# A decoder step on one core: row sums applied by a job of their own, decode attention's values in one burst of matmuls, and matmuls of that stretch tied to places in TensorE's order

## The chip, the cores and the metric

The kernel runs on one core of a Trainium2 chip. The metric is the time of one execution on the device, in microseconds (us). In the profile PE is TensorE, PEld its weight loads, DVE is VectorE, ACT is ScalarE, POOL is GpSimd, SP is SyncE, which here only issues DMAs; a name with a q (SPq) is the queue of that engine, where it waits before it issues. Every engine works through its own instructions in order, and a program that runs at build time decides that order.

## The reference, cut to what matters

One step of a one-layer decoder: 1024 prompt rows and 8 decode rows of width 2048 go through one input projection, sparse attention, an mLSTM and an output projection, all in fp32.

```python
(aq, ak, av, iq, ik, iw, az, mq, mk, mv, mi, mf, mo, mz) = jnp.split(h @ w_in, split_points, axis=-1)

def sparse_attend(q, kg, vg, valid):              # kg, vg: the rows that the index chose
    logits = jnp.einsum('bqhgd,bqjhd->bqhgj', qg, kg) * ATT_SCALE      # 8 heads, 2 kv heads, 128 wide
    p = jax.nn.softmax(jnp.where(valid, logits, -jnp.inf), axis=-1)
    return jnp.einsum('bqhgj,bqjhd->bqhgd', p, vg).reshape(B, Q, ATT_WIDTH)

def dsa_sample(...):                              # 8 decode rows, each chooses 256 of 4097 positions
    _, idx = lax.top_k(scores, topk)
    kg = jnp.where(in_past, cache_k[phys, off], new key)               # paged cache
    vg = jnp.where(in_past, cache_v[phys, off], new value)
    return sparse_attend(q, kg, vg, valid)
# attention's output * silu(az), beside the mLSTM's * silu(mz), goes through w_out; then x + that, RMSNorm
```

## The kernel before, in words

Each fp32 operand is split into a high and a low part, and a product of tiles is three matmuls: high by high, high by low, low by high. The splits of a weight tile (`wraw`, 128x512) are one cast on ACT (L222, tile `wH`) and one subtraction on DVE (L223, tile `wL`), into rings of three buffers each.

**The projection.** The input projection has 61 tiles of 128 columns. Tiles up to 36 are made one after the other by `mm` (L1376, the matmul is L1385) in four quarters of 36 matmuls each; the last two, 35 and 36, run their quarters in the order 2, 3, 0, 1. The activations that these matmuls read are the tiles `xP` (256 columns) and `xQ` and `xR` (388 columns). Tiles 37 to 60 are 12 pairs, made in two phases: 24 steps, numbered 0 to 23, by a product with seven multiplications instead of eight (L1620). Its weights are loaded on the SP queue (L1592, L1595, L1598) into fixed slots and a ring, some are added by a DMA on the POOL queue (L1604), and DVE and ACT split them (L1609, L1610). Steps 0 to 11 store partial sums, and steps 12 to 23 load them back (`pfetch`, L1638, tile `xR` or `ev`) and finish the tiles. Steps 20 to 23 finish the eight tiles of attention's gate az.

**The jobs.** Beside the projection two lanes of jobs are stepped once per quarter. Each job has a first and a last tile and a weight, and a lane runs each job so that its yields come at an even pace between these tiles. On lane 0 the index job chooses positions, the job `att` is the prompt's attention, and `ml` the mLSTM; on lane 1 stand the decode rows' parts. A list scheduler at build time then puts all instructions in order, engine by engine; instructions that are given to `pin` keep the order in which the program issues them.

**Decode attention** (`job_datt`, L1214) runs late in the tiles before 37, after the index job. Sixteen times DVE multiplies a gathered tile of keys `kv` by the query and reduces it (L1264, L1268) into a column group of `lT`. PE then transposes `lT` (L1276), softmax runs on DVE and ACT, PE transposes P (L1296), and 32 matmuls of 4 columns (L1309; an fp32 matmul leaves two records, so the trace has 64) apply the gathered values. The gathers are indirect DMAs on POOL (L1236) into a ring of six buffers. `att` starts when it is done: L577 transposes its values, L614 and L615 are its first softmax.

**Row sums.** `att` writes its output to `attS` in device memory undivided, and the reciprocals of its row sums to `rcS`. They are applied in steps 20 to 23: for each output piece `out` loads them, broadcast over partitions, into a buffer `rb` of the five-buffer ring `ev` (L1665, 24 loads on SP); `use` multiplies the projection's result by them (L1740), takes tanh on ACT (L1744), combines on DVE (L1745) and stores the gate to `gateS` on the POOL queue (L1746), from the same ring. At the end `mixload` reads attention and gate for the output projection (L1352, L1356).

Of the kernel before, what the change touches and what calls it, by code (L numbers as in the profile page):

```python
# [8 lines left out]
F32 = mybir.dt.float32  # L9
# [4 lines left out]
OP = mybir.AluOpType  # L14
# [4 lines left out]
S = 1024  # L19
NB = 8  # L20
# [127 lines left out]
def body(tc, A, stop=None):  # L148
# [1068 lines left out]
    def job_datt():  # L1217
        with tc.tile_pool(name="da", bufs=1, side="right") as pd:
# [37 lines left out]
            for b in range(NB):  # L1256
# [43 lines left out]
            yield 4000  # L1300
            po = bank()
            for b in range(NB):
                if b + 2 < NB:
                    vgs.append(gather("cv", b + 2))
                vg = vgs.pop(0)
                for v in range(2):
                    o = b * 8 + v * 4
                    for u in range(2):
# [3 lines left out]
            ot = pd.tile([128, 8, NB], F32, name="ot")  # L1312
# [4 lines left out]
            V.tensor_tensor(ot, po[:, :64].rearrange("p (b h) -> p h b", b=NB), kn.rearrange("p b h -> p h b"), OP.add)  # L1317
            for x in range(2):
                SY.dma_start(attS[x][:, S:R].rearrange("(a p) b -> p a b", p=128), ot[:, x * 4:x * 4 + 4])
            yield 3000  # L1320

    def att_free():
# [5 lines left out]
    def ix_weight(blocks):  # L1328
# [10 lines left out]
                   Job("dsel", T_AK, 30.0, 2000 + 31 * 1700 + 10000 + 16 * 2800 + 2000, job_dsel),  # L1339
                   Job("datt", T_MQ, 35.5, 7500 + 8 * 5000 + 4000 + 8 * 2500 + 3000, job_datt, ix_free),  # L1340
                   Job("dml", T_G + 0.25, T_G + 10, 20000 + 16 * 2500 + 5000, job_dml)])]
    gateV = gateS.rearrange("(k p) r -> k p r", p=128)
# [280 lines left out]
    keep = {}  # L1623
    parts, free = {}, []
    ahead = [(v, x, c) for v, (_, n) in enumerate(seq) if any(m == n for _, m in seq[:v])
# [14 lines left out]

    def pump(v):
        while free and ahead and ahead[0][0] <= v:
            pfetch()

    def out(v, x, c, ps, sv=None, eng=SC):
# [4 lines left out]
        if not second(v):  # L1650
# [9 lines left out]
            return  # L1660
        rb = None
        if t >= T_AZ:
            cp = min(cn, S - c0)
            rb = evp.tile([128, CN], F32, name="ev")
            SY.dma_start(rb[:, :cp], rcS[(t - T_AZ) // 4][(t - T_AZ) % 4, c0:c0 + cp].partition_broadcast(128))  # L1665
        if (x, c) == (0, 1):
            if t < T_G:
                e = evp.tile([128, CN], F32, name="ev")
                SC.activation(e[:, :cn], ps[:, :cn], AF.Copy, scale=mk)
            else:  # L1670
                e = ps
            use(n, x, c, e, rb)
            return
# [28 lines left out]

    def use(n, x, c, e, rb):
        c0, cn = CH[c]
# [33 lines left out]
        else:  # L1738
            j = t - T_AZ
            V.tensor_tensor(rb[:, :cp], e[:, :cp], rb[:, :cp], OP.mult)  # L1740
            if cp < cn:
                V.tensor_copy(rb[:, cp:cn], e[:, cp:cn])
            h = evp.tile([128, CN], F32, name="ev") if c == 1 and not x else e
            SC.activation(h[:, :cn], e[:, :cn], AF.Tanh, scale=0.5)  # L1744
            V.scalar_tensor_tensor(rb[:, :cn], h[:, :cn], 1.0, rb[:, :cn], OP.add, OP.mult)  # L1745
            G.dma_start(gateS[j * 128:(j + 1) * 128, c0:c0 + cn], rb[:, :cn])  # L1746

    def seed(v, dst, src):
        if second(v):
# [61 lines left out]
    for v, (ph, n) in enumerate(seq):  # L1811
# [331 lines left out]
```

## Time and profile before

| what | us |
|---|---|
| median of 3 runs | 2071.25 |
| range of the runs | 2066.16 to 2073.1 |
| the profiled execution, as timed | 2068.33 |
| its span in the profile | 2066.6 |
| PE busy (97% of the span) | 1998.4 |
| DVE, ACT busy | 1236.9, 976.9 |

The span is that of the instructions in the profile; the execution around it is 1.7 us longer. Matmuls are pipelined and their ends are modelled, so neighbours overlap, and the pace is read from their starts. Where PE is busy for less than a whole window, it waited; where the clock column is under 1.00, TensorE ran part of the window at the lower of its two levels (0.50 in that column).

### The profile page before, as it was taken

Reading aid. Unit: us, or ns where it says so; the run is one execution under the profiler, and the core shown is the slowest. Engines: PE = TensorE matmul, PEld = TensorE weight load, DVE = VectorE, ACT = ScalarE, POOL = GpSimd, SP = SyncE. Lnnn points to the kernel's source line nnn. Section 1 sums busy time; section 2 is a strip of 40 time slices with the busy share of each in tenths; the row PEclk is TensorE's granted clock in tenths of the full one; section 3 lists DMA queues with packets and bytes.
Section 4 is the critical chain, followed back from the end, with each engine's and each line's share of the span. In section 5 each row is a group of like instructions: output and inputs, shape, how many; then the busy total and the mean of one; then the engine's idle time right before and its main releaser. Section 6 shows DMA issues by size and latency. Waiting matters only on the chain.

```text
span 2066.6 us, 34968 instructions
## 1 busy us (share of the span) xinstructions
PE 1998.4 (97%) x12390; PEld 1913.6 (93%) x12390; DVE 1236.9 (60%) x2957; ACT 976.9 (47%) x2061; POOL 249.5 (12%) x318
## 2 busy tenths in 40 slices
PE   9999999999999999988999999989999789999998
PEld 8989999999999999978999999989999689998886
DVE  8492465455555454774666777587777586654331
ACT  8242246753434877113566655465555244433221
POOL 0030111100000000141000000112222111111110
PEclk9999999999999999989999999999999899999999
DMA  7595754532222222456447775697777979567212
GB/s 240 140 341 156 219 177 145 167 110 80 72 72 67 67 62 62 132 157 180 121 121 199 218 199 156 187 284 211 199 201 185 196 246 328 180 210 232 82 51 102
DMA packets 246283, 338.62 MB, mean 164 GB/s; under 512 B 40557, under 2 KB 155181, under 8 KB 246109
## 3 DMA queue, kind: packets, MB, share of 16 engines
q1 hardware_dynamic: 231133, 301.28, 47.3%
q0 software_dynamic: 13824, 33.63, 7.5%
q8 instruction: 97, 1.59, 0.3%
q10 hardware_dynamic: 1152, 1.49, 0.2%
q14 instruction: 77, 0.63, 0.1%
HBM read 253.22 MB, written 83.08 MB: 163 GB/s over the span
## 4 chain that ended last, share of the span: by engine, by line
PE 68%; DMA 6%; DVE 3%; issue 3%; ACT 2%; SPq 0%; POOL 0%; POOLq 0%; DVEq 0%; ACTq 0%
PE pj L1385 20%; PE pj L1620 18%; PE bank L1971 6%; PE bank L2009 6%; PE pj L2009 4%; PE bank L665 2%; PE bank L614 2%; PE bank L463 2%; ACT gt L508 2%; PE bank L656 2%; DMA xP<-in_wa_dram 1%; DMA gateS<-ev 1%; DMA xP<-sS 1%; PE bank L853 1%; DMA wraw<-in_wa_dram 1%
## 5 line engine op out<-in xcount | busy, mean ns | idle before, releaser
L1385 PE MATMUL pj<-xQ,wH 128*128 128x388 f32 (+1 forms) x1832 | 479.4, 340 | 3.8 <-ACT wH L222 1.8
L1620 PE MATMUL pj<-xQ,wH 128*128 128x388 f32 x1344 | 357.1, 344 | 18.6 <-DVE xR L1676 10.8
L222 ACT CAST wH<-wraw 128x512 fp32r<-128x512 f32 (+2 forms) x279 | 169.5, 611 | 418.3 <-PE pj L1385 192.6
L1385 PEld LDWEIGHTS pj<-xQ,wH 128*128 128x128 f32 (+1 forms) x1832 | 326.5, 187 | 7.3 <-ACT wH L222 2.6
L223 DVE TENSOR_TENSOR wL<-wraw,wH 128x512 fp32r<-128x512 f32 (+2 forms) x279 | 193.3, 700 | 228.2 <-ACT wH L222 217.9
L1385 PE MATMUL pj<-xQ,wL 128*128 128x388 f32 (+1 forms) x916 | 310.3, 340 | 1.0 <-DVE wL L223 1.0
L1620 PEld LDWEIGHTS pj<-xQ,wH 128*128 128x128 f32 x1344 | 241.6, 190 | 21.8 <-issue 12.4
L1620 PE MATMUL pj<-xQ,wL 128*128 128x388 f32 x672 | 230.8, 344 | 1.7 <-DVE wL L1610 1.5
L1385 PE MATMUL pj<-xP,wH 128*128 128x256 f32 (+1 forms) x896 | 175.1, 286 | 1.7 <-ACT wH L222 1.1
L1385 PEld LDWEIGHTS pj<-xQ,wL 128*128 128x128 f32 (+1 forms) x916 | 171.3, 187 | 2.4 <-DVE wL L223 1.5
L1620 PE MATMUL pj<-xP,wH 128*128 128x256 f32 x768 | 146.6, 285 | 4.2 <-DVE xR L1678 3.7
L1385 PEld LDWEIGHTS pj<-xP,wH 128*128 128x128 f32 (+1 forms) x896 | 145.2, 189 | 4.3 <-ACT wH L222 1.7
L1610 DVE TENSOR_TENSOR wL<-xP,wH 128x512 fp32r<-128x512 f32 x168 | 115.1, 686 | 51.3 <-ACT wH L1609 47.3
L1609 ACT CAST wH<-xP 128x512 fp32r<-128x512 f32 x168 | 103.0, 618 | 81.6 <-PE pj L1620 75.2
L1385 PE MATMUL pj<-xP,wL 128*128 128x256 f32 (+1 forms) x448 | 126.7, 283 | 3.3 <-DVE wL L223 3.3
L1620 PEld LDWEIGHTS pj<-xQ,wL 128*128 128x128 f32 x672 | 127.1, 189 | 2.9 <-DVE wL L1610 2.6
L1620 PEld LDWEIGHTS pj<-xP,wH 128*128 128x128 f32 x768 | 122.6, 190 | 5.6 <-DVE xR L1678 4.2
L465 ACT ACTIVATE rl<-bank 128x512 f32<-128x512 f32 (+2 forms) x160 | 79.4, 523 | 85.6 <-PE bank L463 54.5
L468 DVE SCALAR_TENSOR_TENSOR s<-rl,wiN,s 128x512 f32<-128x512 f32 (+2 forms) x150 | 94.7, 655 | 33.6 <-ACT rl L465 30.7
L1620 PE MATMUL pj<-xP,wL 128*128 128x256 f32 x384 | 109.0, 284 | 0.0
L508 ACT ACTIVATE gt<-s,sm 128x384 bf16<-128x384 f32 (+5 forms) x96 | 84.6, 881 | 27.3 <-DVE sm L530 21.8
L1385 PEld LDWEIGHTS pj<-xP,wL 128*128 128x128 f32 (+1 forms) x448 | 84.6, 189 | 4.3 <-DVE wL L223 3.6
(460 smaller groups left out, 4218.3 us busy)
## 6 DMA issues: line engine op xcount, KB each, us to landing
wraw<-in_wa_dram SPq DMA_DIRECT2D x166, 256.0 KB
xP<-in_wa_dram SPq DMA_DIRECT2D x120, 256.0 KB
wraw<-in_wo_dram SPq DMA_DIRECT2D x64, 256.0 KB
wraw<-in_wt_dram SPq DMA_DIRECT2D x64, 256.0 KB
part<-ev SPq DMA_DIRECT2D x48, 194.0 KB
xR<-part SPq DMA_DIRECT2D x47, 194.0 KB
y<-in_xT_dram SPq DMA_DIRECT2D x16, 516.0 KB
xS<-y SPq DMA_DIRECT2D x16, 516.0 KB
```

What stands on the lines that cost most here:

```text
L222: a = SC.copy(H[:, s, :cols], raw[:, s, :cols])
L223: return a, V.tensor_tensor(L[:, s, :cols], raw[:, s, :cols], H[:, s, :cols].bitcast(F32), OP.subtract)
L463: PE.matmul(p[:, :cn], qi[:, h % 4, :], ki[x][:, c0:c0 + cn], start=(x == 0), stop=(x == 1))
L465: SC.activation(r[:, :cn], p[:, :cn], AF.Relu)
L468: v = V.scalar_tensor_tensor(s[:, c0:c0 + cn], r[:, :cn], wv, s[:, c0:c0 + cn], OP.mult, OP.add)
L508: SC.activation(junk[:, :W], src[q][:, :W], AF.Sign, bias=bias[:, q:q + 1], scale=scale, accum_out=cnt[:, q:q + 1])
L1385: m = PE.matmul(ps[:cols, :cn], w_[:, k, :cols], xv(kk, xz, c0, cn), start=(n0 == 0 and k == 0 and z == 0), stop=(n0 == n9 and k == 3 and ...
L1609: SC.copy(H, src)
L1610: V.tensor_tensor(L, src, H.bitcast(F32), OP.subtract)
L1620: PE.matmul(ps[:, :n], w_[:, k, :], REG[reg][k](xz), start=(first and k == 0 and z == 0), stop=(last and k == 3 and z == 2), skip_group_ch ...
L1971: PE.matmul(p, w_[:, k, :], x_, start=(n == 0), stop=(n == 47))
L2009: PE.matmul(p, x_[:, bs], w_.rearrange("p a b -> p (a b)"), start=(n == 0 and z == 0), stop=(n == KT - 1 and z == 2))
```

## The change

Four edits. A job `norm` multiplies the attention output by the reciprocals in device memory, between steps 12 and 20: sixteen times it loads a 128x512 piece of `attS` and the broadcast reciprocals, multiplies on DVE, and stores the piece back; loads, multiplications and copies for row sums leave steps 20 to 23. Decode attention's values become 16 matmuls of 256 columns (two per decode row; 32 records) whose left operand `pm` holds P's columns at their places and zeros elsewhere, then a copy and two more transposes; the ring `kv` has 16 buffers. From the end of the key dots to the end of the job, `tied` is set, and the first matmul of each chunk of the projection is pinned, as are the job's transposes and the first matmul of the burst. And a partial-sum buffer that is freed becomes available one call of `pump` later (`just`).

```diff
@@ job_datt
+            pm = pd.tile([128, 2, NB * 72], F32, name="pm")
+            V.memset(pm, 0.0)
-                    g = pd.tile([128, 256], F32, name="kv", bufs=6)
+                    g = pd.tile([128, 256], F32, name="kv", bufs=16)
             vgs = [gather("cv", b) for b in range(2)]
+            tied.append(1)
+            for b in range(2, 6):
+                vgs.append(gather("cv", b))
+                yield 2500
+            yield 2500
+            yield 2500
             p2 = bank()
             for u in range(2):
-                PE.transpose(p2[:64, u * 128:u * 128 + 128], lT[:, u, :], ident)
+                pin(PE.transpose(p2[:64, u * 128:u * 128 + 128], lT[:, u, :], ident))
...
-                        PE.matmul(po[:, o:o + 4], vg[u][:, v * 128:v * 128 + 128], PT[:, u, o:o + 4],
-                                  start=(u == 0), stop=(u == 1))
...
+            for n in range(2 * NB):
+                b, u = n // 2, n % 2
+                m = PE.matmul(po[:64, :256], pm[:, u, b * 64:b * 64 + 64], vgs[b][u], start=(n == 0), stop=(n == 2 * NB - 1))
+                if not n:
+                    pin(m)
+            SC.copy(P, po[:64, :256])
+            yield 3000
+            po = bank()
+            for v in range(2):
+                pin(PE.transpose(po[:, v * 64:v * 64 + 64], P[:, v * 128:v * 128 + 128], ident[:64, :64]))
...
+    def job_norm():
...
+                SY.dma_start(o, row)
+                SY.dma_start(r, rcS[k // 4][k % 4, cs].partition_broadcast(128))
...
+            for n in range(16):
+                o, r, row = nxt.pop(0)
+                pin(V.tensor_tensor(o, o, r, OP.mult))
+                if n + 2 < 16:
+                    nxt.append(fetch(n + 2))
+                yield 1
+                SY.dma_start(row, o)
...
-                   Job("datt", T_MQ, 35.5, 7500 + 8 * 5000 + 4000 + 8 * 2500 + 3000, job_datt, ix_free),
+                   Job("datt", T_MQ, 35.5, 7500 + 8 * 5000 + 10 * 2500 + 3000 + 3000 + 3000, job_datt, ix_free),
+                   Job("norm", T_G + 12.5, T_G + 20, 17, job_norm, lambda: "att" in lanes[0].done)])]
@@ mm
-                if k in between and z == 0:
+                if z == 0 and (k in between or tied and not k):
                     pin(m)
@@ pump, out, use
+        free.extend(just)
+        just.clear()
-            rb = evp.tile([128, CN], F32, name="ev")
-            SY.dma_start(rb[:, :cp], rcS[(t - T_AZ) // 4][(t - T_AZ) % 4, c0:c0 + cp].partition_broadcast(128))
-        later.append(lambda: (use(n, x, c, e, rb), free.append(e)))
+        later.append(lambda: (use(n, x, c, e), just.append(e)))
-            V.tensor_tensor(rb[:, :cp], e[:, :cp], rb[:, :cp], OP.mult)
...
+            h = evp.tile([128, CN], F32, name="ev")
             SC.activation(h[:, :cn], e[:, :cn], AF.Tanh, scale=0.5)
-            V.scalar_tensor_tensor(rb[:, :cn], h[:, :cn], 1.0, rb[:, :cn], OP.add, OP.mult)
+            V.scalar_tensor_tensor(h[:, :cn], h[:, :cn], 1.0, e[:, :cn], OP.add, OP.mult)
@@ the steps
+            lanes[1].ensure("norm")
```

**PE, the transposes of lT.** Before, they stand after the last matmuls (tile `xQ_160`) of the last quarter of tile 35; `pj_9574` is that tile's accumulator.

```order
L1385 MATMUL pj_9574<-xQ_160,wH 128x388 x2
L1385 MATMUL pj_9574<-xQ_160,wL 128x388
L1276 MATMUL bank<-cst,lT 64x128
L1278 MATMUL bank<-onesf,kn 64x1
L1276 MATMUL bank<-cst,lT 64x128
L1296 MATMUL bank<-cst,P 128x64 x2
L1297 MATMUL bank<-cst,pb 128x64
L1309 MATMUL bank<-PT,kv 128x4 x12
```

After (the line numbers are those of the changed kernel: L1428 is the matmul of `mm`, L1284 the transpose), the first of them follows the second quarter of tile 34, whose accumulator is `pj_9322` (`pj_9338` before).

```order
L1428 MATMUL pj_9322<-xQ_160,wH 128x388 x2
L1428 MATMUL pj_9322<-xQ_160,wL 128x388
L1284 MATMUL bank<-cst,lT 64x128
L1286 MATMUL bank<-onesf,kn 64x1
L1428 MATMUL pj_9320<-xP_175,wH 128x256 x2
```

Before, the matmul on `xP_175`, the next quarter of tile 34, follows `xQ_160` there; the transpose has moved ahead of six quarters of 36 matmuls, and all PE work behind it stays behind it.

**DVE, the key dots.** Before, splits of weights (L223) stand between them, one after every second dot or so; from the one behind the third dot on:

```order
L223 TENSOR_TENSOR wL<-wraw,wH 128x512
L1264 TENSOR_TENSOR jk<-kv,qb 128x1024
L1268 TENSOR_REDUCE lT<-jk 128x8
L1264 TENSOR_TENSOR jk<-kv,qb 128x1024
L1268 TENSOR_REDUCE lT<-jk 128x8
L223 TENSOR_TENSOR wL<-wraw,wH 128x512
L1264 TENSOR_TENSOR jk<-kv,qb 128x1024
L1268 TENSOR_REDUCE lT<-jk 128x8
L1264 TENSOR_TENSOR jk<-kv,qb 128x1024
L1268 TENSOR_REDUCE lT<-jk 128x8
L223 TENSOR_TENSOR wL<-wraw,wH 128x512
```

After, from the third dot on (L1266 and L1270 are its two instructions):

```order
L1266 TENSOR_TENSOR jk<-kv,qb 128x1024
L1270 TENSOR_REDUCE lT<-jk 128x8
L223 TENSOR_TENSOR wL<-wraw,wH 128x512
L1266 TENSOR_TENSOR jk<-kv,qb 128x1024
L1270 TENSOR_REDUCE lT<-jk 128x8
L1266 TENSOR_TENSOR jk<-kv,qb 128x1024
L1270 TENSOR_REDUCE lT<-jk 128x8
L1266 TENSOR_TENSOR jk<-kv,qb 128x1024
L1270 TENSOR_REDUCE lT<-jk 128x8
L1266 TENSOR_TENSOR jk<-kv,qb 128x1024
```

One split is left after the third dot, none follows until the sixteenth dot is done; five that stood ahead of the end of the fifteenth dot now come later.

**SP, row sums.** Before, in steps 20 to 23, loads of reciprocals into `ev` wait for DMAs on the POOL queue (DMASW), the gate's stores; outputs of the state (L919, L920) and weight loads (L1592) stand around them.

```order
L919 DMA out_C_p_dram<-C 128x256 [waits DMAHW7_49,DVE_49]
L1638 DMA xR_14855<-part_9568 128x388 [waits DMAHW0_49,DVE_49]
L920 DMA out_n_p_dram<-C 128x1 [waits DMAHW1_49]
L1665 DMA ev<-rcS_104 128x388 [waits DMAHW2_49,DMASW7_49,DMASW5_49]
L1665 DMA ev<-rcS_104 128x256 [waits DMAHW3_49,DMASW4_49,DMASW2_49]
L1665 DMA ev<-rcS_104 128x380 [waits DMAHW4_49,DMASW3_49]
L1665 DMA ev<-rcS_104 128x380 [waits DMAHW5_49,DMASW1_49,DVE_49]
L1592 DMA xP_9845<-in_wa_dram 128x512 [waits DMAHW6_49]
L1592 DMA xP_9845<-in_wa_dram 128x512 [waits DMAHW7_49,DVE_49]
L1665 DMA ev<-rcS_104 128x256 [waits DMAHW0_49,DMASW5_49]
```

After, these loads are gone there, and in steps 12 to 20 the job's DMAs stand (L1360 store, L1349 reciprocals, L1348 attention).

```order
L1360 DMA attS_102<-o 128x512 [waits DMAHW7_49,DVE_49]
L1349 DMA r<-rcS_105 128x512 [waits DMAHW0_49]
L808 DMA rb<-rowS 128x512 [waits DMAHW1_49,DVE_49]
L1348 DMA o<-attS_103 128x512 [waits DMAHW7_49,DMAHW2_49]
L1681 DMA xR_14846<-part_9549 128x388 [waits DMAHW3_49,Activation_49]
L1635 DMA xP_9837<-in_wa_dram 128x512 [waits DMAHW4_49,DVE_49]
L1635 DMA xP_9837<-in_wa_dram 128x512 [waits DMAHW5_49,DVE_49]
L892 DMA hS<-hT 128x4x128 [waits DMAHW6_49,Activation_49]
```

The load L1348 waits for the semaphore of the store L1360 that was issued three rows ahead (DMAHW7), with the weight loads (L1635) queued behind it.

## Rows read from the trace of the kernel before

**Rows 1.** the page, engines: busy us, share of the span, instructions.

```profile
PE 1998.4 (97%) x12390; PEld 1913.6 (93%) x12390; DVE 1236.9 (60%) x2957; ACT 976.9 (47%) x2061; POOL 249.5 (12%) x318
```

**Rows 2.** 20 us windows: length, PE busy, instructions, clock, DMA share, GB/s.

```profile
880.00:900.00 20.00, 16.99 (x104) 1.00 0.74 221
900.00:920.00 20.00, 13.80 (x74) 0.85 0.44 122
920.00:940.00 20.00, 19.55 (x93) 0.55 0.49 140
940.00:960.00 20.00, 17.46 (x109) 1.00 0.72 204
960.00:980.00 20.00, 15.66 (x92) 1.00 0.52 149
```

**Rows 3.** PE timeline at tile 34: start, us, instruction.

```profile
872.95 0.40 PE L1385 MATMUL pj<-xP,wH 128*128 128x256 f32 x2
```

**Rows 4.** DVE timeline, first and fifteenth key dots: start, us, instruction, idle before.

```profile
870.80 1.23 DVE L1264 TENSOR_TENSOR jk<-kv,qb 128x1024 f32<-128x1024 f32 x1 [4.49 <-DMA kv<-in_ck_dram,idxs]
...
875.08 0.68 DVE L223 TENSOR_TENSOR wL<-wraw,wH 128x512 fp32r<-128x512 f32 x1
...
912.03 1.22 DVE L1268 TENSOR_REDUCE lT<-jk 128x8 f32<-128x1024 f32 x1
```

**Rows 5.** PE's waits from 872 to 975 us: total, times, longest.

```profile
PE bank L614 <- DVE st L615: 3.5, 2, 1.8
...
PE bank L1296 <- DVE P L1290: 2.5, 1, 2.5
PE bank L1276 <- DVE lT L1268: 2.4, 1, 2.4
PE bank L577 <- DMA pP<-avS: 2.4, 1, 2.4
```

**Rows 6.** lines from 872.95 to 970.98 us: busy, mean ns, idle before.

```profile
L1236 POOL DMA_INDIRECT kv<-in_cv_dram,idxs x16 | 15.5, 970 | 15.0 <-DVE jk L1264 9.4 <-PE bank L1309 3.0 <-issue 2.5
...
L1309 PE MATMUL bank<-PT,kv 128*128 128x4 f32 x64 | 12.5, 318 | 0.5 <-DVE PT L1299 0.5
```

**Rows 7.** chain of waits, 1580 to 1690 us: start, us, what ended last.

```profile
1586.47 0.44 PE bank L853 x2
...
1588.85 9.17 DMA gateS<-ev
...
1618.26 4.22 DMA xP<-in_wa_dram
1622.55 10.76 DMA wraw<-in_wa_dram
...
1634.69 6.08 DMA gateS<-ev
```

**Rows 8.** SP queue's waits from 1580 to 1705 us.

```profile
SPq L1665 <- DMA gateS<-ev: 31.3, 9, 8.8
...
SPq L1638 <- DMA out_C_p_dram<-C: 7.1, 1, 7.1
```

**Rows 9.** windows: us, busy PE, PEld, DVE, ACT, POOL; clock, DMA share, GB/s.

```profile
1383.00:1590.00 207.00, 207.00 (x1409) 205.03 (x1408) 159.62 (x402) 110.41 (x262) 52.46 (x105) 1.00 0.72 202
...
1600.00:1620.00 20.00, 17.15 (x105) 16.55 (x104) 13.58 (x34) 6.55 (x15) 3.67 (x7) 0.91 0.80 162
1620.00:1640.00 20.00, 11.96 (x77) 11.67 (x76) 6.24 (x13) 4.04 (x8) 2.65 (x4) 0.86 1.08 187
1640.00:1660.00 20.00, 15.18 (x72) 13.94 (x73) 13.83 (x31) 6.68 (x13) 3.63 (x6) 0.80 0.93 303
1660.00:1680.00 20.00, 17.62 (x115) 17.13 (x114) 19.55 (x41) 9.73 (x19) 3.08 (x5) 1.00 0.83 276
```

**Rows 10.** SP queue's waits from 1383 to 1590 us.

```profile
SPq L1638 <- ACT ev L1727: 34.8, 11, 4.5
SPq L1638 <- DVE ev L1729: 25.7, 15, 4.1
```

More of the change, by code (lines that the diff above doesn't have):

```diff
@@ L1293, in job_datt @@
             V.tensor_scalar(pb, onesf[:64], st[:, 4:5], None, OP.mult)
+            yield 2500
+            yield 2500
             p3 = bank()
             for u in range(2):
-                PE.transpose(p3[:, u * 64:u * 64 + 64], P[:, u * 128:u * 128 + 128], ident[:64, :64])
+                pin(PE.transpose(p3[:, u * 64:u * 64 + 64], P[:, u * 128:u * 128 + 128], ident[:64, :64]))
             PE.matmul(p3[:, 128:192], pb, ident[:64, :64], start=True, stop=True)
@@ L1299, in job_datt @@
             V.tensor_copy(PT, p3[:, :192].rearrange("p (a b) -> p a b", a=3))
[L1300 to L1308, printed above, removed]
-                        PE.matmul(po[:, o:o + 4], vg[u][:, v * 128:v * 128 + 128], PT[:, u, o:o + 4],
-                                  start=(u == 0), stop=(u == 1))
+            V.tensor_copy(pm.rearrange("p u (b w) -> p u b w", b=NB)[:, :, :, :8],
+                          PT[:, 0:2].rearrange("p u (b h) -> p u b h", b=NB))
+            for b in range(6, NB):
+                vgs.append(gather("cv", b))
                 yield 2500
-            ot = pd.tile([128, 8, NB], F32, name="ot")
             for b in range(NB):
@@ L1316, in job_datt, with fetch @@
                                 dec[:, T_AV:T_AV + 2, b].unsqueeze(2).to_broadcast([128, 2, 4]), OP.mult)
-            V.tensor_tensor(ot, po[:, :64].rearrange("p (b h) -> p h b", b=NB), kn.rearrange("p b h -> p h b"), OP.add)
+            yield 3000
[6 more added lines that the diff above has]
+            SC.copy(P, po[:64, :256])
+            yield 3000
+            po = bank()
+            for v in range(2):
+                pin(PE.transpose(po[:, v * 64:v * 64 + 64], P[:, v * 128:v * 128 + 128], ident[:64, :64]))
+            ot = pd.tile([128, 8, NB], F32, name="ot")
+            for v in range(2):
+                vs = slice(v * 4, v * 4 + 4)
+                V.tensor_tensor(ot[:, vs], po[:, v * 64:v * 64 + 64].rearrange("p (b h) -> p h b", b=NB)[:, vs],
+                                kn.rearrange("p b h -> p h b")[:, vs], OP.add)
             for x in range(2):
                 SY.dma_start(attS[x][:, S:R].rearrange("(a p) b -> p a b", p=128), ot[:, x * 4:x * 4 + 4])
+            tied.clear()
             yield 3000
+    def job_norm():
+        with tc.tile_pool(name="nr", bufs=3, side="right") as pn:
+            def fetch(n):
+                k, cs = n // 2, slice(n % 2 * 512, n % 2 * 512 + 512)
+                o = pn.tile([128, 512], F32, name="o")
+                r = pn.tile([128, 512], F32, name="r")
+                row = attS[k // 4][(k % 4) * 128:(k % 4 + 1) * 128, cs]
+                SY.dma_start(o, row)
+                SY.dma_start(r, rcS[k // 4][k % 4, cs].partition_broadcast(128))
+                return o, r, row
+            nxt = [fetch(0), fetch(1)]
+            yield 1
[4 more added lines that the diff above has]
+                    nxt.append(fetch(n + 2))
+                yield 1
+                SY.dma_start(row, o)
     def att_free():
@@ L1339, in body @@
                    Job("dsel", T_AK, 30.0, 2000 + 31 * 1700 + 10000 + 16 * 2800 + 2000, job_dsel),
-                   Job("datt", T_MQ, 35.5, 7500 + 8 * 5000 + 4000 + 8 * 2500 + 3000, job_datt, ix_free),
-                   Job("dml", T_G + 0.25, T_G + 10, 20000 + 16 * 2500 + 5000, job_dml)])]
+                   Job("datt", T_MQ, 35.5, 7500 + 8 * 5000 + 10 * 2500 + 3000 + 3000 + 3000, job_datt, ix_free),
+                   Job("dml", T_G + 0.25, T_G + 10, 20000 + 16 * 2500 + 5000, job_dml),
+                   Job("norm", T_G + 12.5, T_G + 20, 17, job_norm, lambda: "att" in lanes[0].done)])]
     gateV = gateS.rearrange("(k p) r -> k p r", p=128)
@@ L1374, in wsrc @@
         return A["wm"][q] if t == 0 else A["wa"][t - 1, q]
+    tied = []
     def mm(ps, cols, t, q, c, H, L, between={}, n0=None, n9=3):
@@ L1623, in body @@
     keep = {}
-    parts, free = {}, []
+    parts, free, just = {}, [], []
     ahead = [(v, x, c) for v, (_, n) in enumerate(seq) if any(m == n for _, m in seq[:v])
@@ L1671, in out @@
                 e = ps
-            use(n, x, c, e, rb)
+            use(n, x, c, e)
             return
@@ L1701, in flush, with use @@
             later.pop(0)()
-    def use(n, x, c, e, rb):
+    def use(n, x, c, e):
         c0, cn = CH[c]
@@ L1739, in use @@
             j = t - T_AZ
-            V.tensor_tensor(rb[:, :cp], e[:, :cp], rb[:, :cp], OP.mult)
-            if cp < cn:
-                V.tensor_copy(rb[:, cp:cn], e[:, cp:cn])
-            h = evp.tile([128, CN], F32, name="ev") if c == 1 and not x else e
+            h = evp.tile([128, CN], F32, name="ev")
             SC.activation(h[:, :cn], e[:, :cn], AF.Tanh, scale=0.5)
-            V.scalar_tensor_tensor(rb[:, :cn], h[:, :cn], 1.0, rb[:, :cn], OP.add, OP.mult)
-            G.dma_start(gateS[j * 128:(j + 1) * 128, c0:c0 + cn], rb[:, :cn])
+            V.scalar_tensor_tensor(h[:, :cn], h[:, :cn], 1.0, e[:, :cn], OP.add, OP.mult)
+            G.dma_start(gateS[j * 128:(j + 1) * 128, c0:c0 + cn], h[:, :cn])
     def seed(v, dst, src):
@@ L1752, in seed @@
             if ring:
-                free.append(e)
+                just.append(e)
         else:
@@ L1902, in body @@
                 free.clear()
+                just.clear()
                 pfetch(True)
```

3 lines of the change are left out of this document (removed).

## The prediction

> **What bounds the kernel now.** I read the page's busy times first, then the windows over the two places that the change touches, then the waits, and the chain and the timelines for their causes. PE is busy for 1998.4 us, 97% of the span [rows 1]. So nearly all of the time is matmul work that the change leaves as it is, and what it can give back is the time in which PE waits or runs at the lower clock. The reader is to see two such places.
>
> Decode attention: in the five windows from 880 to 980 us PE is idle for 3.0, 6.2, 0.45, 2.5 and 4.3 us, 16.5 in all, and at the clock means of 0.85 and 0.55 it does less than its busy time says: 13.80 x 0.15 + 19.55 x 0.45 = 10.9 us [rows 2]. That is 27.4 us lost.
>
> Steps 20 to 23: in the four windows from 1600 to 1680 us PE is busy for 61.9 of 80 us, and at clocks of 0.91, 0.86 and 0.80 it loses 1.5 + 1.7 + 3.0 us more: 18.1 + 6.2 = 24.3 us [rows 9]. The chain goes there through the gate's stores and the loads behind them [rows 7], and SP's queue stood for 31.3 us, 9 times, at L1665 until a gate's store had left the buffer [rows 8].
>
> **Decode attention, part by part.** PE's row is what counts, since all that stands behind the transposes of `lT` now waits for the key dots. PE reaches that place, the start of the third quarter of tile 34, at 872.95 us [rows 3]. The first dot starts at 870.80, where DVE waited for its gathered keys, and the reduction of the fifteenth, which completes the half of `lT` that the first transpose reads, ends at 912.03 + 1.22 = 913.25 [rows 4]. Of seven splits between them two are left in the new order; five of 0.68 us [rows 4] go, so it ends at about 913.25 - 3.4 = 909.9. PE waits from 872.95 to 909.9: **37 us**, in which it did six quarters of work before. Nothing covers it: each engine keeps its order, and the next quarter stands behind the transpose. Earlier gathers (16 buffers) don't help, for the dots follow each other on DVE.
>
> Of the old losses some go, some stay. The wait for `lT` (2.4) is within the 37. The wait for P (2.5) [rows 5] should stay, for the same softmax follows and only some ten rows of matmuls lie between. Of the waits at L577 and L614 (2.4 + 3.5) [rows 5] I keep half, 3: attention's start has moved in PE's order, its loads have had longer. For the lower clock after the 37 us I take 2.1, what the window from 900 to 920 lost around the idle time there, and not the 8.8 of the next window [rows 2], because the 4-column matmuls that ran in that one are gone. So after: 37 + 2.5 + 3 + 2 = 44.5 lost in place of 27.4, **+17**. Ends: nothing but the stall, 37 - 27.4 = +10; the stall and every old clock loss and wait, 37 + 10.9 + 2.5 + 5.9 = 56.3, so +29.
>
> The burst: 16 matmuls leave 32 records, at 0.22 us each by the nearest row of like width (two of L853 take 0.44 [rows 7]) 7.0 us. The 64 small ones are busy for 12.5 us [rows 6], but mostly at the lower clock; at the window's 0.55 that is 6.9 us of full clock. I take 0, between -5.5 and +0.5. Sixteen value gathers of 0.97 us [rows 6] are issued from POOL while the dots end and softmax runs, before the burst reads them. The two transposes more and the copy stand on PE's and ACT's rows in about 0.5 us, an estimate from the 0.22 above and the like; the memset falls where DVE waits for gathers (4.49 [rows 4]).
>
> **Steps 20 to 23.** The 24 loads at L1665 leave SP's queue, and with them the 31.3 us of waits. The weight loads behind them go out earlier. 24 multiplications leave DVE, which was busy for 19.55 of 20 us from 1660 to 1680 [rows 9]. The new buffer for tanh comes from the same ring of five, but is asked for on ACT when the piece is there, later than SP asked before, so the store that must have left it is older; I cost it at nothing, and at one wait of 31.3 / 9 = 3.5 us [rows 8] each time that it isn't. What is late next is the traffic: the state's outputs stay, one of them held SP's queue for 7.1 us [rows 8], and in the window with a DMA share of 1.08 [rows 9] one weight load took 10.76 us where another took 4.22 [rows 7]. The excess of one such load, 6.5 us, is what I leave as lost: 24.3 - 6.5 = **-18**. Ends: all of it, -24; and -10 if the output's 7.1 and the slow load's excess both still reach PE.
>
> **The job in steps 12 to 20.** PE is busy there for 207.00 of 207 us, DVE for 159.62 [rows 9], so 16 multiplications of about 0.68 us, 11 us, lie in DVE's 47 idle ones. Each `attS` load stands in SP's queue behind the store of the same buffer; with the 3.5 us of a gate's store this holds the queue for 16 x 3.5 = 56 us. The edit of the freed part buffers takes waits of 34.8 + 25.7 = 60.5 us from the same queue [rows 10]; PE did not wait with those. The traffic grows: 48 transfers of 256 KB, 12.6 MB in some 190 us, are 66 GB/s on top of 202, so by the same proportion the share of 0.72 [rows 9] becomes 0.96. From below it costs 0 (queue waits as long as before, PE full); from above, if these steps become like the window at a share of 0.83, which lost 2.4 of 20 us [rows 9], 12% of 190, +22. I take one such window, **+2**, as PE shows no wait at all there now.
>
> A rule speaks on the store: the Trainium skill, "DMA: Bandwidth & Descriptors", section "Anatomy of one DMA", has a DMA's semaphore rise only after the last byte is confirmed in the target memory, with a fit of about 2.0 us plus the bytes at 436 GB/s for the GpSimd path. By it a 256 KB store would take about 2.6 us, an estimate, and the job would hold the queue for 42 us, not 56; the gate's stores, smaller, held SP for 3.5 on average and 9.17 in the chain [rows 7], so the trace has it longer.
>
> **The sum.** 17 + 0.5 - 18 + 2 = +1.5 us on the profiled execution's 2068.3: **2070 us**. That execution lies between the runs of 2066.16 and 2073.1, under their median of 2071.25; the forecast is no change against either.
>
> **The rivals.**
>
> *The loss in decode attention stays small and steps 20 to 23 come back whole* (faster). For it: L1665 is the one large wait of that queue, and the stall makes loads and splits of the next tiles ready, so the waits behind it may all go. Against it: the DMA share over 1 and the slow load. Attention +12, steps 20 to 23 -24, the job 0: 2057 us.
>
> *The job's transfers drag steps 12 to 20* (slower). Its place is SP's queue and the DMA engines: each store and load pair holds up the weight loads, and each transfer lands later as the share nears 1. For it: 0.96 by proportion, and the windows at 0.80 to 1.08 are those in which PE waits [rows 9]; against it: these windows also hold the L1665 waits, and the freed buffers give as much queue time back. It decides from the point where a weight load lands later than its split on DVE needs it, which no row of PE shows yet; the whole price of +22 gives 2090, half of it 2079. The Trainium skill, "DMA: Bandwidth & Descriptors", section "Latency and other measured facts", gives HBM access 0.2 us on average and 2 us at high load; the 4.22 and 10.76 us of two like loads agree that traffic lengthens them, by more than that figure.
>
> *The change doesn't free the queue* (slower). The reciprocals' loads go, but the state's outputs and the partial-sum loads still hold the weight loads, or the wait for the ring moves to ACT. For it: 7.1 us on one output; against it: it is one wait against nine. Steps 20 to 23 give 10 instead of 18: 2078 us.
>
> **How the numbers follow.** What can be told from no change here is 0.3%, 6.2 us: below 2065 is faster, above 2077.5 slower. My forecast has 0.42, all of it within 0.3%; the first rival 0.27; the second 0.19, the third 0.12. So faster 0.27, same 0.42, slower 0.31. The likeliest case's own range is 2065 to 2077. The range that should hold the time 8 times in 10 goes from the first rival's 2057 to most of the second's, 2088.
>
> **What would show it.** PE's wait for `lT` at the transposes: about 37 us, from about 873 to 910; under 25 us and the order's reading is wrong. The wait for P: about 2.5. The clock after the stall: back at 1.00 within one 20 us window; if it stays near 0.55 for 20 us, the loss goes toward +29. In steps 20 to 23 no wait of SP for gate's stores and PE idle of under 8 us in four windows that held 18; over 12 and the third rival is true. In steps 12 to 20 PE full in every window; if windows fall to 17 or 18 of 20 with SP waiting at the job's loads, the second rival is true. I am wrong if the stall isn't there, or if PE waits in a stretch that neither of these parts names.

## The result and the profile after

The changed kernel takes 2091.43 us (median of 3 runs, 2088.95 to 2093.56) against 2071.25 before: ratio 1.0102, interval 1.0069 to 1.0135. It is slower by 20 us where I had forecast no change; 2091 lies above the range's end of 2088.

The span and the busy times of the changed kernel, from the page (against [rows 1]):

```profile
span 2087.2 us, 34945 instructions
PE 1994.2 (96%) x12360; PEld 1905.7 (91%) x12360; DVE 1234.7 (59%) x2944; ACT 974.1 (47%) x2062; POOL 234.2 (11%) x318
```

PE is busy for 4 us less in a span that is 21 us longer. So it waits more, and the question is where. Decode attention in the changed kernel, the same windows as [rows 2] and one ahead of them (length, PE busy, instructions, clock, DMA share, GB/s):

```profile
860.00:880.00 20.00, 11.85 (x76) 0.92 0.80 224
880.00:900.00 20.00, 0.00 (x0) 0.50 0.68 221
900.00:920.00 20.00, 9.22 (x44) 0.64 0.14 41
920.00:940.00 20.00, 20.00 (x105) 0.91 0.22 66
940.00:960.00 20.00, 20.00 (x131) 1.00 0.57 180
960.00:980.00 20.00, 19.51 (x116) 1.00 0.66 180
```

A whole window without a matmul. PE's waits from 860 to 1000 us (total, times, longest) and PE's and DVE's timelines give the wait its cause; "issue" says only that the profile shows no releaser:

```profile
PE bank L1284 <- issue: 37.2, 1, 37.2
PE bank L1306 <- DVE P L1298: 1.0, 1, 1.0
```

```profile
871.52 0.33 PE L1428 MATMUL pj<-xQ,wL 128*128 128x388 f32 x1
909.09 0.40 PE L1284 MATMUL bank<-cst,lT 128*64 128x128 f32 x1 [37.24 <-issue]
```

```profile
870.38 1.22 DVE L1266 TENSOR_TENSOR jk<-kv,qb 128x1024 f32<-128x1024 f32 x1 [4.40 <-DMA kv<-in_ck_dram,idxs]
...
907.77 1.22 DVE L1270 TENSOR_REDUCE lT<-jk 128x8 f32<-128x1024 f32 x1
```

DVE's fifteenth reduction ends at 908.99, and the transpose starts at 909.09. This is the stall of the forecast, 37.2 us where it said 37. The wait for P fell to 1.0 (2.5 in [rows 5]), and the 32 records of the burst are busy for 7.1 us, by the same view as [rows 6]:

```profile
L1323 PE MATMUL bank<-kv,pm 128*64 128x256 f32 x32 | 7.1, 381 | 0.0
```

The other two places in the changed kernel, with three windows of the first between them (length, busy PE, PEld, DVE, ACT, POOL, clock, DMA share, GB/s):

```profile
1410.00:1600.00 190.00, 182.33 (x1214) 178.31 (x1213) 140.32 (x347) 93.01 (x222) 44.88 (x89) 1.00 0.84 245
1470.00:1490.00 20.00, 16.84 (x116) 16.46 (x115) 12.82 (x34) 8.37 (x20) 4.02 (x9) 1.00 0.89 256
1490.00:1510.00 20.00, 17.76 (x116) 17.24 (x115) 15.56 (x39) 10.31 (x27) 4.62 (x10) 1.00 0.83 229
1510.00:1530.00 20.00, 18.54 (x123) 17.80 (x122) 14.23 (x36) 7.65 (x18) 4.36 (x9) 1.00 0.80 217
1600.00:1720.00 120.00, 108.51 (x682) 106.36 (x681) 82.78 (x180) 52.19 (x112) 25.04 (x45) 0.97 0.75 192
```

and the kernel before, for the same two places:

```profile
1410.00:1600.00 190.00, 190.00 (x1291) 188.31 (x1290) 145.44 (x364) 102.14 (x240) 48.57 (x97) 1.00 0.73 199
1600.00:1720.00 120.00, 99.82 (x582) 96.87 (x581) 82.13 (x170) 45.48 (x89) 16.83 (x29) 0.93 0.86 241
```

In steps 12 to 20 PE now waits, 7.7 us of 190, nearly all of it in three windows of 20 us, with the DMA share up from 0.73 to 0.84. From 1600 to 1720 it waits less, but not by the 18 of the forecast.

The table adds up what PE lost, stretch by stretch: over windows of 10 us the idle time, and the busy time multiplied by what the clock was short of 1.00. It is worked out from the profiled run of each kernel; the stretches are fixed in time, while kernels drift against each other by up to 53 us (the steps' last matmul on `xQ` and `wH` starts at 1673.6 in e9 and at 1726.2 in e7), a profiled run can lie some us off its kernel's median (that of e3, 2072.39, is the slowest of its ten runs), and an edit lets the scheduler reorder instructions elsewhere too, so stretches that no edit touches scatter by some us (1000 to 1410: 10 to 17).

| kernel | 860-1000 | 1000-1410 | 1410-1600 | 1600-1720 | median us | ratio to before, interval |
|---|---|---|---|---|---|---|
| before | 27.5 | 10.3 | 0.0 | 24.7 | 2071.25 | |
| the change | 45.6 | 12.4 | 7.7 | 13.9 | 2091.43 | 1.0102, 1.0069 to 1.0135 |
| e1_values_only | 44.9 | 12.5 | 0.6 | 24.2 | 2088.96 | 1.0110, 1.0079 to 1.0140 |
| e2_norm_only | 29.0 | 12.2 | 7.5 | 14.1 | 2072.70 | 1.0020, 1.0005 to 1.0034 |
| e3_untied | 24.1 | 16.1 | 7.6 | 17.9 | 2065.57 | 0.9979, 0.9964 to 0.9995 |
| e4_norm_small | 45.3 | 15.8 | 1.2 | 16.4 | 2082.13 | 1.0065, 1.0039 to 1.0092 |
| e5_np_rows | 30.6 | 16.4 | 7.3 | 3.9 | 2062.60 | 0.9967, 0.9951 to 0.9984 |
| e6_own_ring | 30.1 | 12.3 | 0.0 | 26.8 | 2075.99 | 1.0037, 1.0023 to 1.0050 |
| e7_few_mults | 46.6 | 15.5 | 8.0 | 16.9 | 2093.24 | 1.0112, 1.0085 to 1.0138 |
| e8_ring_np | 30.2 | 11.6 | 0.0 | 14.3 | 2058.44 | 0.9942, 0.9921 to 0.9963 |
| e9_tied_later | 12.5 | 16.0 | 6.0 | 3.7 | 2041.45 | 0.9862, 0.9842 to 0.9881 |
| e10_norm_spread | 26.8 | 17.2 | 1.9 | 4.3 | 2060.83 | 0.9964, 0.9951 to 0.9977 |
| e11_ring_later | 16.7 | 15.4 | 0.0 | 13.7 | 2047.56 | 0.9887, 0.9861 to 0.9913 |
| e12_before_np | 24.1 | 10.1 | 0.0 | 13.4 | 2055.03 | 0.9933, 0.9910 to 0.9956 |

The change against before: +18.1, +2.1, +7.7, -10.8, +1.5 behind 1720 us and -1.6 ahead of 860, in all 17.0 of the 20.6 by which the span grew. The 1.5 behind 1720 is the first wait of the output projection, which the kernel before has ahead of 1720; so the gain in steps 20 to 23 is 9 to 11.

### The profile page after: what moved, and what is told of

Read it like the earlier page. It is cut to its first block, busy times and chain, and to the rows that moved or that the text cites. A ratio compares the mean times of both kernels' runs of the same rounds, so it can differ in the third digit from the quotient of the medians.

```text
span 2087.2 us, 34945 instructions
## 1 busy us (share of the span) xinstructions
PE 1994.2 (96%) x12360; PEld 1905.7 (91%) x12360; DVE 1234.7 (59%) x2944; ACT 974.1 (47%) x2062; POOL 234.2 (11%) x318
## 4 chain that ended last, share of the span: by engine, by line
PE 64%; DMA 8%; issue 4%; DVE 3%; ACT 3%; SPq 0%; POOL 0%; POOLq 0%; DVEq 0%; ACTq 0%
PE pj L1428 20%; PE pj L1663 17%; PE bank L2010 7%; PE bank L2048 6%; PE pj L2048 4%; PE bank L665 2%; PE bank L614 2%; DMA xP<-in_wa_dram 2%; PE bank L463 2%; ACT gt L508 2%; PE bank L656 1%; DMA xP<-sS 1%; DMA rb<-rowS 1%; DMA out_C_p_dram<-C 1%; DMA xR<-xS 1%
## 5 line engine op out<-in xcount | busy, mean ns | idle before, releaser
L1428 PE MATMUL pj<-xQ,wH 128*128 128x388 f32 (+1 forms) x1832 | 481.1, 341 | 2.8 <-ACT wH L222 1.9
L223 DVE TENSOR_TENSOR wL<-wraw,wH 128x512 fp32r<-128x512 f32 (+2 forms) x279 | 194.6, 705 | 240.3 <-ACT wH L222 234.0
L1428 PEld LDWEIGHTS pj<-xQ,wH 128*128 128x128 f32 (+1 forms) x1832 | 327.6, 188 | 7.0 <-ACT wH L222 3.2
L1428 PE MATMUL pj<-xQ,wL 128*128 128x388 f32 (+1 forms) x916 | 311.0, 341 | 1.0 <-DVE wL L223 1.0
L1428 PE MATMUL pj<-xP,wH 128*128 128x256 f32 (+1 forms) x896 | 175.4, 286 | 0.7 <-ACT xP L291 0.7
L1428 PEld LDWEIGHTS pj<-xQ,wL 128*128 128x128 f32 (+1 forms) x916 | 171.8, 188 | 2.6 <-DVE wL L223 1.6
L1428 PEld LDWEIGHTS pj<-xP,wH 128*128 128x128 f32 (+1 forms) x896 | 145.1, 189 | 3.1 <-ACT xP L291 1.2
L1428 PE MATMUL pj<-xP,wL 128*128 128x256 f32 (+1 forms) x448 | 126.8, 283 | 0.0
L2010 PE MATMUL bank<-mH,wH 128*128 128x392 f32 x256 | 86.4, 342 | 1.5 <-ACT wH L222 1.5
```

The costliest lines, as they stand in the source:

```text
L223: return a, V.tensor_tensor(L[:, s, :cols], raw[:, s, :cols], H[:, s, :cols].bitcast(F32), OP.subtract)
L2010: PE.matmul(p, w_[:, k, :], x_, start=(n == 0), stop=(n == 47))
```

## The experiments

**Each half alone.** e1 leaves out the job and the later freeing of buffers; the row sums are back in steps 20 to 23.

```diff
-                   Job("norm", T_G + 12.5, T_G + 20, 17, job_norm, lambda: "att" in lanes[0].done)])]
+            rb = evp.tile([128, CN], F32, name="ev")
+            SY.dma_start(rb[:, :cp], rcS[(t - T_AZ) // 4][(t - T_AZ) % 4, c0:c0 + cp].partition_broadcast(128))
```

> The burst, the 16 buffers and the tied TensorE order alone; the row sums stay in steps 20 to 23 as before and freed part buffers are available at once. Theory A (two traces compared: the first weight split of step 7 comes 19.5 us later than before, and the wait at the first transpose is 37.2 us): decode attention alone costs 18 to 20 us, so 2088 to 2092. Theory B (most of the stall is soaked up by waits further on that it makes needless, and the row-sum job is what costs): under 2080.

2088.96: theory A. The stall is there, and nothing further on soaks it up. Its wait at the first transpose:

```profile
PE bank L1284 <- issue: 36.6, 1, 36.6
```

e2 keeps the job and the later freeing, and gives decode attention back its old form.

```diff
-            tied.append(1)
-                        g = pd.tile([128, 256], F32, name="kv", bufs=16)
+                        g = pd.tile([128, 256], F32, name="kv", bufs=6)
```

> The job for the row sums and the later freeing of part buffers, with decode attention as before. Theory N (the delay of the changed kernel grows from 19.4 to 31.5 us over steps 14 to 18 and falls to 21.4 by step 23): the job costs 12 us in steps 15 to 18 and steps 20 to 23 give back 10, so +2, 2070 to 2076. Rival (the growth in steps 15 to 18 is a matter of how the stalled kernel's schedule fell, not of the job): 8 to 12 us faster than before, 2058 to 2063.

2072.70, theory N: 7.5 us lost in steps 12 to 20 and 10.6 won in steps 20 to 23, as in the change; with the stall gone the losses remain, so they are the job's own. The later freeing is not their cause: e6 and e8 below keep it without the job and lose 0.0 there.

**The ties.** e3 takes out one line.

```diff
-            tied.append(1)
```

> As the change, but the projection's matmuls are not pinned while the values are worked on; the transposes of lT then stand behind the last quarter of tile 35 in TensorE's order, as before. Theory A (the place of the transposes is the cost): the 37 us wait shrinks to under 5 and the kernel is 18 to 22 us faster than the changed one, 2069 to 2073. Rival (the burst itself, its copy and its transposes cost as much as the pins): 2080 or more.

2065.57: theory A, and 26 us below the change, more than I expected. The transposes are back at their old place and the wait there is 2.4 us, as it was before:

```profile
PE bank L1283 <- DVE lT L1270: 2.4, 1, 2.4
```

The burst itself costs nothing that shows.

**What in the job costs.** e4 keeps the number of its transfers and cuts their bytes to an eighth.

```diff
-                k, cs = n // 2, slice(n % 2 * 512, n % 2 * 512 + 512)
-                o = pn.tile([128, 512], F32, name="o")
-                r = pn.tile([128, 512], F32, name="r")
+                k, cs = n // 2, slice(n % 2 * 512, n % 2 * 512 + 64)
+                o = pn.tile([128, 64], F32, name="o")
+                r = pn.tile([128, 64], F32, name="r")
```

> As the change, but the job handles 64 of each 512 columns: 16 loads, 16 broadcasts, 16 multiplications and 16 stores as before with an eighth of the bytes, and seven eighths of the row sums left out. Theory Q (the job costs 12 us because its loads hold SP's queue until the store before them has landed): 2086 to 2092, since the waits remain, only somewhat shorter. Theory T (the job costs by its traffic of 12.6 MB and its 11 us on DVE): 10 to 12 us faster than the change, 2079 to 2081.

2082.13, 9 us below the change; theory T had 10 to 12. The loss from 1410 to 1600 falls to 1.2. SP's waits there at the job's loads for the store ahead of them, in the change first, then in e4:

```profile
SPq L1348 <- DMA attS<-o: 20.2, 11, 4.3
```

```profile
SPq L1348 <- DMA attS<-o: 20.9, 11, 5.0
```

The queue is held as long as before and PE is hardly late: the holding is not what costs. e4 cut the multiplications along with the bytes, so e7 moves all bytes and multiplies only 64 columns.

```diff
-                pin(V.tensor_tensor(o, o, r, OP.mult))
+                pin(V.tensor_tensor(o[:, :64], o[:, :64], r[:, :64], OP.mult))
```

> As the change, with all loads and stores of the job whole, but each of its multiplications only over 64 of 512 columns (so seven eighths of the row sums are left out): 0.2 us on DVE in place of 0.68. Theory T (the job costs by its traffic): the loss from 1410 to 1600 us stays at 6 to 8 us and the time at 2088 to 2092. Theory V (it costs by the 11 us more on DVE, which shifts the mLSTM's chain): the loss falls to 1 or 2, as in e4_norm_small, and the time to 2081 to 2084.

2093.24, 1 us above theory T's range, and 8.0 us lost, within it: it is the bytes that move, not DVE. Its window:

```profile
1410.00:1600.00 190.00, 183.62 (x1208) 178.26 (x1207) 134.14 (x349) 90.38 (x218) 43.27 (x87) 0.99 0.83 243
```

DVE is busy for 6 us less than in the change, with PE as late. By which transfer PE becomes late is not settled: DVE's waits for weight loads grew from 2.7 to 16.1 us,

```profile
DVE xP L1838 <- DMA xP<-in_wa_dram: 2.7, 4, 0.9
```

```profile
DVE xP L1876 <- DMA xP<-in_wa_dram: 16.1, 7, 3.6
```

(before, then the change, 1410 to 1600), but they are still 10.7 in e4, where PE loses little. PE's own longest wait there is at the mLSTM's transposes, for ACT's normalized output, first in the change, then in e4:

```profile
PE bank L889 <- ACT hm L881: 3.2, 1, 3.2
```

```profile
PE bank L889 <- ACT hm L881: 0.8, 1, 0.8
```

With two shorter ones at L855, 4.0 of the 7.7 us are waits of the mLSTM's own matmuls, and not of the projection's.

**What steps 20 to 23 still lose.** In the change SP issues four stores of the mLSTM's normalizer there, each 128 pieces of 4 bytes (SP's timeline: start, us, instruction):

```profile
1618.57 0.34 SPq L919 DMA_DIRECT2D out_C_p_dram<-C  x1
1618.96 0.87 SPq L920 DMA_DIRECT2D out_n_p_dram<-C  x1
...
1632.49 0.34 SPq L919 DMA_DIRECT2D out_C_p_dram<-C  x1
1632.88 0.42 SPq L920 DMA_DIRECT2D out_n_p_dram<-C  x1
```

The other two follow at 1641.98 and 1644.88. Behind the two shown the DMA engines are busy while they move little (windows of the change, columns as above):

```profile
1620.00:1625.00 5.00, 5.00 (x31) 5.00 (x30) 1.50 (x3) 1.89 (x6) 2.01 (x4) 1.00 0.96 142
1625.00:1630.00 5.00, 4.45 (x30) 3.94 (x28) 0.69 (x1) 2.60 (x6) 2.01 (x4) 1.00 0.76 85
1635.00:1640.00 5.00, 5.00 (x33) 4.95 (x32) 4.41 (x9) 2.85 (x6) 0.00 (x0) 1.00 0.88 44
```

A share of 0.76 to 0.96 at 44 to 142 GB/s, where 1410 to 1600 moves 245 at 0.84. The chain of waits in the change goes there through a slow weight load (start, us):

```profile
1621.94 8.41 DMA xP<-in_wa_dram
```

e5 stores the normalizer as four rows, on top of e3.

```diff
-                SY.dma_start(A["n_p"][h].rearrange("(p o) -> p o", o=1), C[:, h, 256:257])
+            pN = bank()
+            PE.transpose(pN[:4, :128], C[:, :, 256], ident)
+            nT = pm.tile([4, 128], F32, name="nT", bufs=1)
+            SC.copy(nT, pN[:4, :128])
+            SY.dma_start(A["n_p"], nT)
```

> As e3_untied, but the mLSTM's normalizer (out_n_p, 4 heads of 128 values) is transposed on TensorE and stored as 4 rows of 512 bytes in one DMA, in place of four DMAs that write 128 pieces of 4 bytes each. Theory O (these four writes keep the DMA engines busy at 44 to 85 GB/s for some 5 us each, and the weight loads behind them come late; that is what steps 20 to 23 still lose after the row sums left them): the loss from 1600 to 1720 us, 17.9 in e3_untied, falls to 8 to 11, and the time to 2055 to 2060. Rival (what is lost there is the mLSTM's own chain and the loads of the output projection): within 3 us of e3_untied, 2063 to 2068.

The loss from 1600 to 1720 falls from 17.9 to 3.9, further than theory O had it. The time, 2062.60, is only 3 us below e3's and above what I expected; the two intervals overlap, for e3's runs reach from 2058 to 2072, and in the profiled runs e5 loses 6.5 more than e3 from 860 to 1000, which its edit does not touch. So e12 makes the same edit in the kernel before:

> The kernel before with one edit: the normalizer stored as 4 rows of 512 bytes, as in e5_np_rows. Theory O (of the 24.7 us that steps 20 to 23 lose, the four stores of 4-byte pieces have 10 to 14): 2055 to 2059. Rival (the row sums' loads alone make the loss, the small stores only show once these are gone): 2065 to 2069.

2055.03, theory O: 15 us below the runs of before beside it (2070.42), and 13.4 lost in place of 24.7. The window behind its one store, issued at 1609.50:

```profile
1610.00:1615.00 5.00, 5.00 (x31) 5.00 (x30) 3.29 (x7) 3.40 (x7) 1.61 (x3) 1.00 0.93 265
```

and DVE's waits for weight loads from 1600 to 1720, before and in e12:

```profile
DVE xP L1838 <- DMA xP<-in_wa_dram: 18.4, 2, 12.1
```

```profile
DVE xP L1842 <- DMA xP<-in_wa_dram: 5.2, 1, 5.2
```

These waits fall in the other two pairs as well, from 13.6 to 3.7 (e3, e5) and from 8.7 to 2.1 (e6 and e8 below). So the stores' cost reaches PE through loads that come late. Whether it is the 4-byte pieces or the number of stores is not separated; the edit changes both.

e6 asks whether the row sums cost steps 20 to 23 only because the gate's stores hold their ring: it is e3 without the job, and applies them there again, from a ring of their own.

```diff
-            rb = evp.tile([128, CN], F32, name="ev")
+                rbp.append(mctx.enter_context(tc.tile_pool(name="rbp", bufs=3, side="right")))
+            rb = rbp[0].tile([128, CN], F32, name="rb")
-            G.dma_start(gateS[j * 128:(j + 1) * 128, c0:c0 + cn], rb[:, :cn])
+            G.dma_start(gateS[j * 128:(j + 1) * 128, c0:c0 + cn], h[:, :cn])
```

> As e3_untied, without the job: the row sums are applied in steps 20 to 23 again, but their loads go into a ring of three buffers of their own, which no store to the gate holds; all 24 loads and multiplications are there. Theory H (what steps 20 to 23 lost before was SP's queue held at these loads by the gate's stores): they lose about as little as with the job, 14 to 18 us in place of 24.7, and steps 12 to 20 lose nothing instead of 7.6, so 6 to 9 us below e3_untied, 2056 to 2060. Rival (it was the loads' traffic and the multiplications themselves): steps 20 to 23 lose 22 or more, 2065 to 2070.

2075.99, and 26.8 lost: theory H misses. But the hold was not wholly gone, only its releaser changed. SP's waits from 1580 to 1705 us in e6 (31.3 on the gate's stores in [rows 8]):

```profile
SPq L1690 <- DVE ev L1770: 16.3, 9, 5.3
```

e8 puts e5's edit on top of e6.

> e6_own_ring and e5_np_rows together. If theories H and O hold and their losses are separate: steps 12 to 20 lose nothing and steps 20 to 23 about 8, so 2046 to 2052, faster than both kernels of the change. If the two are one loss (loads late by either): 2055 to 2060, as the better of the two alone.

2058.44, above the lower guess and within the other: 14.3 lost in steps 20 to 23, as much as in e12 with the old ring (13.4). SP's waits at these loads over the same window, in e12 and in e8:

```profile
SPq L1669 <- DMA gateS<-ev: 24.5, 10, 4.9
```

```profile
SPq L1694 <- DVE ev L1774: 13.5, 11, 5.3
```

The loss does not follow the hold: e12 is held for 24.5 us and loses 13.4, e8 for 13.5 and loses 14.3; the kernel before is held for 31.3 and loses 24.7, e6 for 16.3 and loses 26.8. So the length of the hold isn't it. The normalizer's stores have 11 to 14 us (24.7 to 13.4, 17.9 to 3.9, 26.8 to 14.3), and taking the row sums out of these steps 9 to 11 (24.7 to 13.9, 26.8 to 17.9, 14.3 to 3.9); the two add. Whether the latter is the loads, the multiplications or their waits stays open.

**Versions.** e9 keeps the ties, and moves the transposes to where the dots are done; e5's edit is in it.

```diff
+            for _ in range(7):
+                yield 5000
             tied.append(1)
-                   Job("datt", T_MQ, 35.5, 7500 + 8 * 5000 + 10 * 2500 + 3000 + 3000 + 3000, job_datt, ix_free),
+                   Job("datt", T_MQ, 37.5, 7500 + 8 * 5000 + 7 * 5000 + 10 * 2500 + 3000 + 3000 + 3000, job_datt, ix_free),
```

> The change whole, with the normalizer stored as rows as in e5_np_rows, and with seven yields more between the key dots and the transposes (the job's end set from 35.5 to 37.5), so that in TensorE's order the transposes of lT stand some seven quarters later than in the change; all ties stay. Theory A (only the place was wrong: with the place right the ties hide the waits): the 37 us wait falls under 3, the loss from 860 to 1000 us to 8 to 16 (before 27.5, untied 24 to 31), and the time to 2045 to 2054. Rival (a late start of the prompt's attention, or the ties, costs as much elsewhere): 2060 to 2066, no better than e5_np_rows.

**2041.45 us**, ratio 0.9862: better than theory A had it, 29 us faster than before and 50 faster than the change. Of the 29, the normalizer's rows alone are worth 15 in e12. PE's waits from 860 to 1000 us no longer have one for `lT`:

```profile
PE pj L1434 <- issue: 3.0, 7, 0.7
PE pj L1434 <- ACT ev L358: 2.7, 1, 2.7
PE bank L1312 <- DVE P L1304: 1.6, 1, 1.6
PE bank L1313 <- DVE pb L1307: 0.4, 1, 0.4
```

and the window that was half at the lower clock [rows 2] is nearly whole:

```profile
920.00:940.00 20.00, 17.99 (x111) 0.97 0.69 176
```

12.5 us are lost there, against 45.6 with the ties at the old place and 24 to 31 in the runs without them (e3, e5, e6, e8, e10). So the place was what was wrong. That the ties themselves are worth having is not shown: e9 moved the place and kept the ties, and no run has the later place without them.

e10 is e5 with the job over a longer stretch.

```diff
-                   Job("norm", T_G + 12.5, T_G + 20, 17, job_norm, lambda: "att" in lanes[0].done)])]
+                   Job("norm", T_G + 10, T_G + 20.5, 17, job_norm, lambda: "att" in lanes[0].done)])]
```

> As e5_np_rows, with the job for the row sums due from tile 47 to 57.5 in place of 49.5 to 57. Theory T (traffic per time is what costs in steps 12 to 20): the same bytes over a longer stretch, so the loss from 1410 to 1600 us falls from 7.3 to 3 to 5 us, but the stretch from 1320 to 1410, whose DMA engines are full already, may lose more; 2058 to 2063. Rival (each of the job's transfers costs, however spread): within 1 us of 7.3.

1.9 us lost from 1410 to 1600, better than expected, and 12.6 from 1320 to 1410 (13.2 in e5). The time, 2060.83, can't be told from e5's. Joined with e9 it was not run.

e11 is e9 without the job, with e6's ring.

> As e9_tied_later, but with the row sums in steps 20 to 23 and their own ring, as in e8_ring_np, and no job. By the sums of the stretches so far: 860 to 1000 us 8 to 16 as e9_tied_later, steps 12 to 20 nothing, steps 20 to 23 14 as e8_ring_np: 2042 to 2050. Against e9_tied_later this tells what the job is worth when the normalizer's stores are out of the way: theory P (7 lost in steps 12 to 20 against 10 won in steps 20 to 23): e9 is 3 us the faster.

2047.56, within the forecast. The median of e9 is 6 us lower, but the intervals overlap, and from 860 to 1000, where the two kernels have the same code, their profiled runs differ by 4.2. What the job is worth is not settled: e3 with it is 10 us faster than e6 without it, e5 with it 4 us slower than e8 without it. By the stretches all three pairs say the same: the job costs 6 to 8 us in steps 12 to 20 and saves 9 to 10 in steps 20 to 23, a gain of 1 to 4.

## Why the prediction was wrong, point by point

- **The stall and decode attention: right.** 37 us forecast, 37.2 measured; +17 for the part, +18.1 measured. The details differ: the wait for P was 1.0, not 2.5, the waits at L577 and L614 came to 0.9, not 3, and the clock cost 4.3, not 2.1 (the 45.6 of the table less 41.3 us of idle time). That these small terms came to nearly the sum forecast for them is luck. The clock was at its lower level from 876.8 to 914.3 us, most of it while PE stood idle, and once more from 921.1 to 924.5.
- **Steps 20 to 23: the step that failed.** "24.3 - 6.5 = -18" gave nearly the whole loss to the row sums' loads, because SP's queue waited at them for 31.3 us. It gave back 10.8, at the end "-10" of the range, which I had as the third rival. SP's waits for the gate's stores are gone there, as forecast; PE's idle time from 1600 to 1720 was 11.5 (20.2 before), between the signs of under 8 and over 12. What stayed was named as late next, "the state's outputs", and priced by one slow load, 6.5 us; e12 puts the normalizer's four stores at 11 us. The prediction took the place where a queue waits for the cause of the loss; e6, e8 and e12 show that a hold shorter by 11 to 15 us changes nothing in the loss. The loads themselves, with their multiplications, had 9 to 11.
- **The job in steps 12 to 20: mis-sized.** +2 forecast, +7.7 measured, within 0 to +22. "PE shows no wait at all there now" was the reason for the low value. A full PE says that there is no loss yet, not how much slack is left. The term's mechanism in the text, SP's queue, was wrong as well: 20.2 us of holding in place of 56, and e4 shows that it is harmless; the second rival's traffic is what e7 confirms, and its sign was there: windows of 16.8, 17.8 and 18.5 us of 20. The share rose to 0.84, not the 0.96 by proportion.
- **The holding of the queue.** SP waited 20.2 us in all, 11 times: 20.2 / 11 = 1.8 us each for 256 KB, and 20.9 / 11 = 1.9 for 32 KB in e4. My 3.5 from the gate's stores was too long. The estimate of 2.6 us a store worked out from the Trainium skill, "DMA: Bandwidth & Descriptors", section "Anatomy of one DMA", mostly a fixed part that waits for the write's confirmation, was nearer. That section is about DMAs issued from GpSimd, and these stores were issued from SP; what was measured is SP's wait, which starts some time after the store. That the wait is alike at an eighth of the bytes agrees with a mostly fixed part.
- **The rivals were priced one at a time.** Each slower one moved a single term and left the others at their likeliest values, 2078 and 2079 to 2090. Both came true together: 7.2 us less gain and 5.7 us more drag. With 0.6 more in decode attention and 5.6 that no term named (2.0 of it in the other stretches of the table, the rest not placed) that is 19.1 us, from 2070 to the 2089 of the profiled execution; the median lies 2.5 above that one.

## What to carry to other kernels

Read a planned order against the time that the engine behind it needs: a pinned instruction whose operand takes another engine 37 us costs these 37 us, and with the same pins some seven quarters later the stretch loses 12.5 us in place of 45.6. Where a queue waits and a stretch loses time, look too for windows in which the DMA engines are busy at a low rate, and price each cause by taking it away alone. And where a forecast is a difference of large terms, let the range hold two of them going wrong the same way.

## What the runs showed of the hardware

Four stores of 512 bytes each, as 128 pieces of 4 bytes, cost 11 to 14 us of matmul time against one store of four rows of 512 bytes (before and e12, e3 and e5, e6 and e8). Behind two of them in the change the DMA engines were at a share of 0.76 to 0.96 with 44 to 142 GB/s, and behind the one store in e12 at 0.93 with 265; DVE's waits for weight loads fell from 18.4 to 5.2 us from before to e12. The Trainium skill, "DMA: Bandwidth & Descriptors", section "Specifications", names 512 bytes as the least for full rate. The trace agrees in direction, and what it adds is the price. PE's wait of 37 us, most of it at the lower clock, cost 4.3 us of clock besides itself: about 5 us after PE resumed at 909.1 the clock was back (914.3), with one more fall of 3.4 us.
